# Hybrid attention and PEER block: the dense pass takes tiles 1 to 3 of the first half, and all four tiles of the second half are gathered

## The chip, the cores and the metric

The kernel runs on one core of a Trainium2 chip. The metric is the device time of one launch in microseconds, the median of three runs. A profiled execution of the same program gives the trace.

## The reference

One block of a decoder on 1024 tokens of width 1024: differential attention and a state-space mixer side by side, then a retrieval network (PEER) that picks 128 of 16384 single-neuron experts for each token. The change touches the retrieval network alone:

```python
q = (tb @ w_query).reshape(-1, 8, 2, 128)
sc = jnp.einsum('thjd,jkd->thjk', q, sub_keys)
val, idx = lax.top_k(sc, 16)
...
top_s, pos = lax.top_k(cand_s, 16)
eidx = jnp.take_along_axis(cand_i, pos, axis=-1)
g = jax.nn.softmax(top_s, axis=-1)
act = jax.nn.gelu(jnp.einsum('thkd,td->thk', expert_u[eidx], tb), approximate=False)
wts = g * act
return jnp.einsum('thk,thkd->td', wts, expert_v[eidx])
```

Then `x = layer_norm(ALPHA * x + gate2 * y_ffn, ln2_g, ln2_b)`.

## The kernel before

The 1024 tokens are taken in two halves of 512, each of four tiles of 128 tokens (tiles 0 to 3 and 4 to 7). `main` runs attention, the mixer, the projections and the first layer norm of the first half, then of the second; each half ends with `scores`, which multiplies by `w_query` and the sub-keys and writes the scores of all tiles to DRAM (`sc_d`).

After that a tile goes through `route`: VectorE searches the 16 best of each head (`top16`), adds candidates and picks experts by one-hot passes (`oh`, `fe`). Then a tile goes one of two ways.

A **gathered** tile (`gathered`): GpSimd gathers one row of `peer_u` per token for each of 128 selections (a u row: 128 tokens by 1024 values, 512 KB, tile `grow`), and VectorE multiplies it with the tokens' h2 and sums (line 1125). Then 128 v rows of `peer_v` are gathered, one for each token, and TensorE adds them up with the weights (`ps_y`). `finish` makes the last layer norm.

A **dense** tile: `spread` turns its experts and weights into a full table of gates, token by 16384 experts, as products of two one-hot rows (`first_k` on VectorE, `second_k` on GpSimd, `ps_gate` on TensorE), which goes to DRAM (`g_d`). `dense` then runs over all 128 blocks of 128 experts: `ps_u` with the block of `peer_u`, GELU, times the gates (`act_t`, read back as `gl`), and `ps_v` with the block of `peer_v`. One block is called a dense step here. Every weight is split into a high and a low part (`whi` on ScalarE, `wlo` on VectorE, line 220).

`few = 2, 3` says how many tiles of each half are gathered: tiles 0, 1 and 4, 5, 6; tiles 2, 3 and 7 are dense. The dense loop is `lead` = 12 steps ahead with `ps_u`; before the first multiplication with gates it issues all that is missing of the routing (`await_gates`), tile 7 coming first in the second half.

The order of work: `drive` records the main stream and after each piece of it as much of the other work as a credit allows (`ratio`, `ratio1`), gathering (`side`) and routing (`urgent`) by turns given in `share`. Every engine then executes its instructions in one fixed order, so an instruction that waits holds all behind it on its engine. Gathered rows lie in the `row` buffers (6, shared with scores, one-hots and norm rows) and, in the dense stage, in 7 `row2` buffers; `gs`, which collects gates for DRAM, has one buffer. A v row is multiplied `rows_by` = 4 rows after its gather was issued.

## Time and profile before

| | |
|---|---|
| median of three runs | 4839.74 us (4829.25 to 4852.5) |
| profiled execution | 4822.5 us, span 4820.7 us |
| TensorE busy | 4016.2 us (83%) |
| VectorE busy | 2974.3 us (62%) |
| ScalarE busy | 1423.7 us (30%) |
| GpSimd busy | 1881.6 us (39%) |
| DMA | 1134.14 MB, mean 235 GB/s |
| mean granted TensorE clock | 0.909 |

The span is the time from the first to the last instruction of the profiled execution. A share of busy time is a mean over stages that differ: the first half ends near 1100 us, the second half near 2540 us, the dense steps run from 3010 to about 4480 us, and the last gathered tile ends the program. So the time is read stage by stage.

### The profile page before, as it was taken

How to read it: one execution, taken by the hardware profiler on the slowest of the kernel's cores; microseconds unless marked ns; L12 is line 12 of the kernel's file. 1: busy time of each engine (PE TensorE's matmuls, PEld its weight loads, DVE VectorE, ACT ScalarE, POOL GpSimd, SP SyncE). 2: the span in 40 equal slices, each digit the busy share in tenths (PEclk: the TensorE clock that was granted, in tenths of full speed). 3: DMA queues.
4: the chain of work that ended last, by engine and by line, in shares of the span. 5: the costliest groups of instructions: out<-in, count | busy, mean ns of one | idle time of the engine just before them, and what ended most of it. 6: DMA issues, size and time to landing. Idle time of an engine off the chain costs nothing.

```text
span 4820.7 us, 52596 instructions
## 1 busy us (share of the span) xinstructions
PE 4016.2 (83%) x17996; PEld 2752.8 (57%) x17996; DVE 2974.3 (62%) x6965; ACT 1423.7 (30%) x2340; POOL 1881.6 (39%) x1720
## 2 busy tenths in 40 slices
...
GB/s 282 105 70 119 73 107 103 137 147 101 170 163 163 300 232 236 264 266 276 191 303 256 319 195 92 308 311 297 275 280 285 355 333 325 272 284 314 361 393 349
DMA packets 443648, 1134.14 MB, mean 235 GB/s; under 512 B 141852, under 2 KB 164532, under 8 KB 443380
## 3 DMA queue, kind: packets, MB, share of 16 engines
...
q8 instruction: 143, 2.34, 0.2%
q14 instruction: 125, 1.02, 0.1%
...
## 4 chain that ended last, share of the span: by engine, by line
PE 54%; DVE 18%; DMA 13%; issue 8%; POOL 5%; ACT 2%; SPq 1%; DVEq 0%; ACTq 0%; POOLq 0%
PE ps_u L269 9%; PE ps_v L1330 8%; PE ps_y L1290 7%; DVE grow L1125 5%; PE ps_x L269 5%; DMA grow<-in_peer_v,ej 5%; PE ps_b L269 4%; DMA grow<-in_peer_u,ei 3%; PE ps_z L269 3%; PE ps_g L269 2%; POOL grow L1182 2%; DVE wlo L220 2%; POOL second_k L1259 2%; PE ps_vT L269 2%; PE ps_pq L269 2%
## 5 line engine op out<-in xcount | busy, mean ns | idle before, releaser
L1182 POOL DMA_INDIRECT grow<-in_peer_u,ei x640 | 856.0, 1337 | 983.9 <-DVE grow L1125 312.0
L1182 POOL DMA_INDIRECT grow<-in_peer_v,ej x640 | 681.8, 1065 | 731.1 <-PE ps_y L1290 589.0
L219 ACT CAST whi<-wraw 128x1024 fp32r<-128x1024 f32 x498 | 519.9, 1047 | 1390.7 <-PE ps_u L269 548.9
L220 DVE TENSOR_TENSOR wlo<-wraw,whi 128x1024 fp32r<-128x1024 f32 x498 | 607.2, 1220 | 483.5 <-ACT whi L219 431.7
L1125 DVE SCALAR_TENSOR_TENSOR grow<-grow,gh 128x1024 f32<-128x1024 f32 x640 | 771.3, 1220 | 96.9 <-DMA grow<-in_peer_u,ei 95.4
L1290 PE MATMUL ps_y<-grow,own 128*32 128x512 f32 x2560 | 614.6, 636 | 83.7 <-DMA grow<-in_peer_v,ej 63.5
L269 PE MATMUL ps_u<-hhi,whi 128*128 128x384 f32 x1024 | 363.4, 355 | 48.2 <-ACT whi L219 40.8
L269 PE MATMUL ps_u<-hhi,wlo 128*128 128x384 f32 x1024 | 361.7, 353 | 44.2 <-DVE wlo L220 44.0
L1259 POOL TENSOR_SCALAR second_k<-iota_c,at 128x128 f32<-128x128 f32 x384 | 308.6, 814 | 228.3 <-PE ps_gate L1290 181.4
L983 POOL DMA_DIRECT2D h2s_d<-bighi x8 | 4.5, 561 | 915.3 <-ACT bighi L245 915.3
L1152 DVE COPY own<-wt 128x4 f32<-128x4 f32 x160 | 28.6, 182 | 536.5 <-PE ps_y L1290 532.7
L269 PE MATMUL ps_u<-hlo,whi 128*128 128x384 f32 x1024 | 354.9, 347 | 0.0
L1290 PEld LDWEIGHTS ps_y<-grow,own 128*32 128x32 f32 x2560 | 89.9, 111 | 405.7 <-DMA grow<-in_peer_v,ej 203.3
L1290 PE MATMUL ps_gate<-first_k,second_k 128*128 128x128 f32 x768 | 192.7, 386 | 107.7 <-POOL second_k L1259 62.0
L1330 PE MATMUL ps_v<-whi,ehi 128*128 128x512 f32 x768 | 225.2, 411 | 68.0 <-ACT whi L219 49.2
L1330 PE MATMUL ps_v<-wlo,ehi 128*128 128x512 f32 x768 | 256.4, 407 | 23.3 <-DVE wlo L220 23.3
L269 PEld LDWEIGHTS ps_u<-hhi,whi 128*128 128x128 f32 x1024 | 199.8, 195 | 118.2 <-ACT whi L219 52.3
L269 PEld LDWEIGHTS ps_u<-hhi,wlo 128*128 128x128 f32 x1024 | 199.7, 195 | 97.6 <-DVE wlo L220 65.8
L1330 PE MATMUL ps_v<-whi,elo 128*128 128x512 f32 x768 | 249.3, 400 | 0.0
L1290 PEld LDWEIGHTS ps_gate<-first_k,second_k 128*128 128x128 f32 x768 | 152.2, 250 | 157.7 <-POOL second_k L1259 102.4
L1330 PEld LDWEIGHTS ps_v<-whi,ehi 128*128 128x128 f32 x768 | 142.9, 193 | 128.3 <-ACT whi L219 59.9
L269 PEld LDWEIGHTS ps_u<-hlo,whi 128*128 128x128 f32 x1024 | 199.7, 195 | 17.8 <-issue 14.3
...
## 6 DMA issues: line engine op xcount, KB each, us to landing
wraw<-in_w_in SPq DMA_DIRECT2D x160, 512.0 KB, 3.7
wraw<-in_peer_uT SPq DMA_DIRECT2D x128, 512.0 KB, 6.3
wraw<-in_peer_v SPq DMA_DIRECT2D x128, 512.0 KB, 6.6
wada<-in_w_adaT SPq DMA_DIRECT2D x48, 512.0 KB, 6.6
g_d<-gs ACTq DMA_DIRECT2D x48, 512.0 KB, 4.3
gl<-g_d SPq DMA_DIRECT2D x48, 512.0 KB, 13.2
...
wraw<-in_w_ssd SPq DMA_DIRECT2D x32, 512.0 KB, 3.7
```

The lines of the kernel that those rows point to most:

```text
L219: nc.scalar.copy(hi, raw)
L220: i = nc.vector.tensor_tensor(lo, raw, hi.bitcast(F32), op=ALU.subtract)
L269: i = self.nc.tensor.matmul(ps, w[x][:, k, :], r[y][:, k, :], start=k + n == 0, stop=k == kk - 1 and n == 2)
L983: nc.gpsimd.dma_start(self.h2s_d[part][:, k, :], big[k][part][:, g0:])
L1125: nc.vector.scalar_tensor_tensor(u, u, 1.0, h2, op0=ALU.mult, op1=ALU.mult, accum_out=act[:, k : k + 1])
L1152: nc.vector.tensor_copy(own[:, :, OWN - 1].rearrange("p (h r) -> p h r", h=2), wt[:, b * n : b * n + n].rearrange("p (h r) -> p h r", h=2) ...
L1182: self.nc.gpsimd.indirect_dma_start(out=r, out_offset=None, in_=table, in_offset=bass.IndirectOffsetOnAxis(ap=ei[:, k : k + 1], axis=0),)
L1259: nc.gpsimd.tensor_scalar(second, self.iota_c, at[:, 1, k : k + 1], None, op0=ALU.is_equal)
L1290: return op(*args, **kw)
L1330: nc.tensor.matmul(acc[2 * tt + c], prev[x][:, tt * P : tt * P + P], v[y].rearrange("p k c -> p (k c)")[:, c * 512 : c * 512 + 512], start ...
```

## The change

Tiles 1, 2 and 3 are dense and tiles 0, 4, 5, 6 and 7 are gathered (`few = 1, 4`): the dense pass needs no tile of the second half. Routing of a half is planned before its scores, and `route` waits while recording until the scores it needs are recorded (`scored`). The dense loop is 2 steps ahead instead of 12. Gathered rows have buffers of their own, 4 in the two halves and 10 in the dense stage; the other rows share 4, `gs` and `ys` among them; `finish` and `rows_out` load their rows one by one, and h2 is made in place. Turns are one gathering to one routing step in the halves (two to one before), and a v row waits 2 rows in the halves and 6 in the dense stage. In DRAM the gates lie so that a load moves 4 KB runs and a write 256-byte runs; before it was the other way.

```diff
--- before.py
+++ after.py
@@ -48,22 +48,22 @@
 class Block:
     n_two = 12
     n_four = 5
-    n_row = 6
-    n_row2 = 7
-
-    lead = 12
+    n_row = 4
+    n_grow = 4, 10
+
+    lead = 2
     ahead = 1000000
-    ratio = 0.95
+    ratio = 0.9
     ratio1 = 1.1
 
-    share = 2, 4
+    share = 1, 4
     lag = 6, 2
 
     behind_by = 2
 
-    rows_by = 4
-
-    few = 2, 3
+    rows_by = 2, 6
+
+    few = 1, 4
     banks = {"pj0": 1, "pj1": 1, "ms": 2, "S": 3, "gate": 1}
 
     def __init__(self, ctx, tc, a, out):
...
@@ -132,7 +132,7 @@
         self.h2s_d = [dr.tile([P, KD, TH - P * self.few[0]], F32R, name=f"h2s_d{i}") for i in range(2)]
 
         self.g_d = {
-            hb * 4 + t: dr.tile([P, 16, P, 8], F32, name=f"g_d{hb * 4 + t}")
+            hb * 4 + t: dr.tile([P, 16, 16, 64], F32, name=f"g_d{hb * 4 + t}")
             for hb in range(2) for t in range(self.few[hb], 4)
         }
 
...
@@ -347,8 +347,9 @@
         self.mod2 = m
 
     def row(self, name):
-        if self.dp and name == "grow":
-            return self.dp.tile([P, D], F32, name=name, tag="row2", bufs=self.n_row2)
+        if name == "grow":
+            pool, n = (self.dp, self.n_grow[1]) if self.dp else (self.gp, self.n_grow[0])
+            return pool.tile([P, D], F32, name=name, tag="grow", bufs=n)
         return self.gp.tile([P, D], F32, name=name, tag="row", bufs=self.n_row)
 
 
...
@@ -966,36 +967,37 @@
             if b in (2, 4, 6):
                 yield from islice(fill, 1)
         yield from fill
-        rows = []
-        for src, off in ((a["ln1_g"], 0), (a["ln1_b"], 0), (self.mod_d, D), (self.mod_d, 0)):
-            rows.append(self.row("lnr"))
-            nc.sync.dma_start(rows[-1], bcast_rows(src, off, D))
-        self.late = v, rows
+        self.late_v = v
         self.h2T = self.join(big)
-        g0 = P * self.few[hb]
-        if hb:
-            for part in range(2):
-                for k in range(KD):
-                    nc.gpsimd.dma_start(self.h2x[part][:, k, TH - P * self.few[0] :], big[k][part][:, g0:])
-        else:
+        if hb == 0:
             for k in range(KD):
                 for part in range(2):
-                    nc.gpsimd.dma_start(self.h2s_d[part][:, k, :], big[k][part][:, g0:])
+                    nc.gpsimd.dma_start(self.h2s_d[part][:, k, :], big[k][part][:, P * self.few[0] :])
 
     def rows_out(self, hb):
 
-        nc = self.nc
-        v, rows = self.late
+        nc, a, v = self.nc, self.a, self.late_v
+
+        def load(*srcs):
+            rows = []
+            for src, off in srcs:
+                rows.append(self.row("lnr"))
+                nc.sync.dma_start(rows[-1], bcast_rows(src, off, D))
+            return rows
+
+        rows = load((a["ln1_g"], 0), (a["ln1_b"], 0))
         for tt in range(4):
             sl = slice(hb * TH + tt * P, hb * TH + tt * P + P)
             nc.vector.tensor_tensor(v[tt], v[tt], rows[0], op=ALU.mult)
             nc.vector.tensor_tensor(v[tt], v[tt], rows[1], op=ALU.add)
             nc.sync.dma_start(self.x1_d[sl, :], v[tt])
-            if tt < self.few[hb]:
-                h2 = self.row("h2")
-                nc.vector.tensor_tensor(h2, v[tt], rows[2], op=ALU.mult)
-                nc.vector.tensor_tensor(h2, h2, rows[3], op=ALU.add)
-                nc.sync.dma_start(self.h2_d[sl, :], h2)
+            yield
+        rows = load((self.mod_d, D), (self.mod_d, 0))
+        for tt in range(self.few[hb]):
+            sl = slice(hb * TH + tt * P, hb * TH + tt * P + P)
+            nc.vector.tensor_tensor(v[tt], v[tt], rows[0], op=ALU.mult)
+            nc.vector.tensor_tensor(v[tt], v[tt], rows[1], op=ALU.add)
+            nc.sync.dma_start(self.h2_d[sl, :], v[tt])
             yield
 
     def first_half(self):
...
@@ -1056,6 +1059,8 @@
         val, idx = small("val"), small("idx", U32)
         fi = idx.bitcast(F32)
         for half in range(2):
+            while self.scored < (tile_no // 4, 8 * half + 8):
+                yield 0.0
             s = self.row("scr").rearrange("p (a b) -> p a b", a=8)
             nc.sync.dma_start(s, self.sc_d[tile_no, :, half * 8 : half * 8 + 8, :])
             for i in range(8):
...
@@ -1136,13 +1141,14 @@
         self.claimed = False
 
         n = 2 * OWN
+        by = self.rows_by[self.dp is not None]
         rows = deque()
-        for k in range(P + self.rows_by):
+        for k in range(P + by):
             if k < P:
                 b, r, half = k // n, k % n // 2, k % 2
                 rows.append(self.gather(a["peer_v"], ej, b * n + half * OWN + r))
-            if k >= self.rows_by and k % 2:
-                j = k - self.rows_by
+            if k >= by and k % 2:
+                j = k - by
                 b, r = j // n, j % n // 2
                 if r == 0:
                     yield from self.claim("side")
...
@@ -1188,35 +1194,42 @@
     def finish(self, t0, y, src=None):
 
         nc, a = self.nc, self.a
-        x1, rows = self.row("gx1"), []
-        nc.sync.dma_start(x1, self.x1_d[t0 : t0 + P, :])
-        for r, off in ((self.mod_d, 2 * D), (a["ln2_g"], 0), (a["ln2_b"], 0)):
-            rows.append(self.row("gr2"))
-            nc.sync.dma_start(rows[-1], bcast_rows(r, off, D))
+
+        def load(src):
+            r = self.row("gr2")
+            nc.sync.dma_start(r, src)
+            return r
+
+        gate = load(bcast_rows(self.mod_d, 2 * D, D))
         if src is None:
-            nc.vector.tensor_tensor(y, y, rows[0], op=ALU.mult)
+            nc.vector.tensor_tensor(y, y, gate, op=ALU.mult)
         else:
             for c, ps in enumerate(src):
                 cs = slice(c * 512, c * 512 + 512)
-                nc.vector.tensor_tensor(y[:, cs], ps, rows[0][:, cs], op=ALU.mult)
-        nc.vector.scalar_tensor_tensor(y, x1, ALPHA, y, op0=ALU.mult, op1=ALU.add)
+                nc.vector.tensor_tensor(y[:, cs], ps, gate[:, cs], op=ALU.mult)
+        nc.vector.scalar_tensor_tensor(
+            y, load(self.x1_d[t0 : t0 + P, :]), ALPHA, y, op0=ALU.mult, op1=ALU.add
+        )
         mean, rs = self.moments([y], self.gp, "ln2")
-        nc.vector.scalar_tensor_tensor(y, y, mean, rows[1], op0=ALU.subtract, op1=ALU.mult)
-        nc.vector.scalar_tensor_tensor(y, y, rs, rows[2], op0=ALU.mult, op1=ALU.add)
+        nc.vector.scalar_tensor_tensor(
+            y, y, mean, load(bcast_rows(a["ln2_g"], 0, D)), op0=ALU.subtract, op1=ALU.mult
+        )
+        nc.vector.scalar_tensor_tensor(
+            y, y, rs, load(bcast_rows(a["ln2_b"], 0, D)), op0=ALU.mult, op1=ALU.add
+        )
         nc.sync.dma_start(self.out[t0 : t0 + P, :], y)
 
 
-    def routing(self, hb):
+    def routing(self, tiles):
 
         nc, gp = self.nc, self.gp
-        tiles = range(4 * hb, 4 * hb + 4)
-        for t in reversed(tiles) if hb else tiles:
-            while len(self.picked) == 3:
+        for t in tiles:
+            while len(self.picked) == 2:
                 yield 0.0
             yield from self.route(t)
             fe, g = self.routed
-            if t < 4 * hb + self.few[hb]:
-                ei, ej = [gp.tile([P, NSEL], I32, name=x, tag=x, bufs=3) for x in ("ei", "ej")]
+            if t % 4 < self.few[t // 4]:
+                ei, ej = [gp.tile([P, NSEL], I32, name=x, tag=x, bufs=2) for x in ("ei", "ej")]
                 nc.vector.tensor_copy(ei, fe)
                 yield from self.claim("urgent")
                 ps = self.psum("ps_ej", tag="gate")
...
@@ -1261,20 +1274,17 @@
             if k >= self.behind_by:
                 n = k - self.behind_by
                 if n % 4 == 0:
-                    spare = next(self.spare, None)
-                    if spare is None:
-                        yield from self.claim("urgent")
-                    ps = self.psum("ps_gate", tag=spare or "gate")
+                    yield from self.claim("urgent")
+                    ps = self.psum("ps_gate", tag="gate")
                 first, second = ready.popleft()
                 self.inline(nc.tensor.matmul, ps[:, n % 4 * P : n % 4 * P + P], second, first, start=True, stop=True)
                 if n % 8 == 0:
-                    gs = gp.tile([P, D], F32, name="gs", tag="gs", bufs=1).rearrange("p (i t) -> p t i", t=8)
+                    gs = self.row("gs").rearrange("p (i t) -> p t i", t=8)
                 if n % 4 == 3:
                     nc.scalar.copy(gs[:, n % 8 - 3 : n % 8 + 1, :], ps.rearrange("p (t i) -> p t i", t=4))
-                    if spare is None:
-                        self.claimed = False
+                    self.claimed = False
                 if n % 8 == 7:
-                    nc.scalar.dma_start(self.g_d[t][:, n // 8], gs.rearrange("p t i -> p i t"))
+                    nc.scalar.dma_start(self.g_d[t][:, :, n // 8], gs.rearrange("p t (b i) -> p b (i t)", b=16))
             if k % 2:
                 yield 1.0
 
...
@@ -1294,8 +1304,7 @@
         nc, a, dp = self.nc, self.a, self.dp
         tiles = list(self.g_d)
         n = P * len(tiles)
-        tags = ("S", "S", "S", "ms", "ms", "pj1")[: 2 * len(tiles)]
-        self.spare = cycle(tags)
+        acc = [self.psum("ps_v", tag=t) for t in ("S", "S", "S", "ms", "ms", "pj1")[: 2 * len(tiles)]]
         ts, prev = deque(), None
         for e in range(P + self.lead + 1):
             if e < P:
...
@@ -1309,14 +1318,15 @@
             if f < 0:
                 continue
             if f < P:
+                if f == 0:
+                    while self.missing:
+                        self.step("side" if self.claimed == "side" else "urgent")
                 if f % 8 == 0:
-                    if f == 0:
-                        self.await_gates()
-                        self.spare = iter(())
-                        acc = [self.psum("ps_v", tag=t) for t in tags]
                     gt = dp.tile([P, len(tiles) * 16, 8, 8], F32, name="gl", tag="gl", bufs=2)
                     for i, t in enumerate(tiles):
-                        nc.sync.dma_start(gt[:, i * 16 : i * 16 + 16], self.g_d[t][:, :, f : f + 8, :])
+                        nc.sync.dma_start(
+                            gt[:, i * 16 : i * 16 + 16].rearrange("p g i t -> p g (i t)"), self.g_d[t][:, f // 8]
+                        )
                 t = ts.popleft()
                 tv = t.rearrange("p (i t) -> p i t", t=8)
                 nc.vector.tensor_tensor(tv, tv, gt[:, :, f % 8, :], op=ALU.mult)
...
@@ -1376,9 +1381,9 @@
             else:
                 self.h2x = self.first_half()
             yield from self.post_norm(hb, big, fill)
+            self.scored = hb, 0
+            self.plan(hb)
             yield from self.scores(hb, self.h2T)
-            if hb == 0:
-                self.plan(0)
 
     def step(self, only=None):
 
...
@@ -1440,9 +1445,7 @@
 
     def plan(self, hb):
 
-        while self.urgent:
-            self.step()
-        self.urgent = self.routing(hb)
+        self.urgent = chain(self.urgent or (), self.routing(range(4 * hb, 4 * hb + 4)))
 
     def run(self):
         tc = self.tc
...
@@ -1461,10 +1464,7 @@
             self.wp = c.enter_context(tc.tile_pool(name="wp", bufs=1))
             with tc.tile_pool(name="bp", bufs=1) as self.bp, tc.tile_pool(name="mp", bufs=1) as self.mp:
                 self.drive(self.main(), self.ratio, self.lag[0])
-                while self.urgent:
-                    self.step()
             with tc.tile_pool(name="dp", bufs=1) as self.dp:
-                self.plan(1)
                 self.drive(self.dense(self.h2x), self.ratio1, self.lag[1])
                 while self.side or self.urgent:
                     self.step()
```

What GpSimd executes from tile 7's gates to the end, before: the first rows are the end of tile 1's v rows among tile 3's gates (`second_k`), then tile 7's gates, then three gathered tiles.

```order
L1182 DMA grow<-in_peer_v,ej 128x1024 x30
L1259 TENSOR_SCALAR second_k<-iota_c,at 128x128 x2
L1182 DMA grow<-in_peer_v,ej 128x1024 x2
L1259 TENSOR_SCALAR second_k<-iota_c,at 128x128 x6
L1182 DMA grow<-in_peer_v,ej 128x1024 x26
L1259 TENSOR_SCALAR second_k<-iota_c,at 128x128 x166
L1182 DMA grow<-in_peer_u,ei 128x1024 x128
L1182 DMA grow<-in_peer_v,ej 128x1024 x128
L1182 DMA grow<-in_peer_u,ei 128x1024 x128
L1182 DMA grow<-in_peer_v,ej 128x1024 x128
L1182 DMA grow<-in_peer_u,ei 128x1024 x128
L1182 DMA grow<-in_peer_v,ej 128x1024 x128
```

The same place after, from the v rows of tile 0 (`hhi` and `hlo` are the dense pass's tokens):

```order
L1188 DMA grow<-in_peer_v,ej 128x1024 x39
L1009 DMA hlo<-h2s_d_117 128x8x384
L1009 DMA hhi<-h2s_d_116 128x8x384
L1188 DMA grow<-in_peer_v,ej 128x1024 x85
L1272 TENSOR_SCALAR second_k<-iota_c,at 128x128 x128
L1188 DMA grow<-in_peer_u,ei 128x1024 x128
L1188 DMA grow<-in_peer_v,ej 128x1024 x128
L1188 DMA grow<-in_peer_u,ei 128x1024 x128
L1188 DMA grow<-in_peer_v,ej 128x1024 x128
L1188 DMA grow<-in_peer_u,ei 128x1024 x128
L1188 DMA grow<-in_peer_v,ej 128x1024 x128
L1188 DMA grow<-in_peer_u,ei 128x1024 x128
L1188 DMA grow<-in_peer_v,ej 128x1024 x128
```

The gates in front of the dense steps are now tile 3's, and four gathered tiles stand behind them instead of three.

TensorE at the same place, before: the last v products of tile 1 (`ps_y`), gates of tile 3, keys and gates of tile 7, then the first products with `peer_v`.

```order
L1290 MATMUL ps_y<-grow,own_103 32x512 x8
L1290 MATMUL ps_gate<-first_k,second_k 128x128 x40
L1290 MATMUL ps_key<-ident,keys 128x128 x2
L1290 MATMUL ps_key<-ident,g 128x128
L1290 MATMUL ps_gate<-first_k,second_k 128x128 x128
L1330 MATMUL ps_v<-whi,ehi 128x512 x2
L1330 MATMUL ps_v<-wlo,ehi 128x512 x2
L1330 MATMUL ps_v<-whi,ehi 128x512 x2
L1330 MATMUL ps_v<-wlo,ehi 128x512 x2
```

TensorE after, where keys and gates of tile 3 stand behind the first block of `ps_u`:

```order
L269 MATMUL ps_u<-hhi,whi 128x384
L269 MATMUL ps_u<-hlo,whi 128x384
L269 MATMUL ps_u<-hhi,wlo 128x384
L1300 MATMUL ps_key<-ident,keys 128x128 x2
L1300 MATMUL ps_key<-ident,g 128x128
L1300 MATMUL ps_gate<-first_k,second_k 128x128 x128
L269 MATMUL ps_u<-hhi,whi 128x384
L269 MATMUL ps_u<-hlo,whi 128x384
L269 MATMUL ps_u<-hhi,wlo 128x384
L269 MATMUL ps_u<-hhi,whi 128x384
```

The products of a gathered tile no longer stand there; tile 0's are now spread over the end of the second half's main stream. On VectorE the u rows of a tile stand before among 24.5 and 26 dense steps (tiles 6 and 5) and now among 19, 16.5 and 16.5 (tiles 4, 5 and 6), the route of the following tile with them each time.

## Rows read from the trace of the kernel before

**Rows 1.** Windows by stage: us, busy time (instructions) of PE, PEld, DVE, ACT, POOL.

```profile
1100.00:1500.00 400.00, 353.22 (x1501) 238.56 (x1500) 388.50 (x1318) 168.69 (x353) 80.58 (x68) 0.88 0.43 139
1500.00:2100.00 600.00, 569.83 (x2702) 363.26 (x2700) 366.97 (x685) 236.40 (x384) 308.13 (x283) 0.97 0.73 248
2100.00:2540.00 440.00, 322.41 (x1482) 258.09 (x1483) 365.32 (x844) 112.42 (x145) 265.59 (x240) 0.84 0.80 263
2540.00:3010.00 470.00, 313.31 (x1250) 167.88 (x1250) 201.11 (x755) 78.88 (x88) 255.74 (x324) 0.71 0.62 217
3010.00:3400.00 390.00, 304.18 (x1376) 253.49 (x1375) 357.12 (x882) 100.96 (x137) 200.46 (x143) 0.93 0.90 300
3400.00:3700.00 300.00, 291.72 (x1342) 172.16 (x1342) 84.95 (x127) 67.21 (x93) 127.07 (x110) 0.99 0.85 288
3700.00:4050.00 350.00, 295.46 (x1392) 249.18 (x1391) 262.89 (x408) 95.18 (x131) 203.56 (x140) 0.93 0.95 334
4050.00:4390.00 340.00, 339.61 (x1557) 200.92 (x1556) 89.24 (x129) 75.41 (x104) 142.95 (x127) 1.00 0.83 283
4390.00:4640.00 250.00, 96.96 (x409) 74.30 (x408) 211.65 (x373) 28.68 (x40) 163.55 (x133) 0.70 0.95 356
4640.00:4821.00 181.00, 128.28 (x490) 18.38 (x488) 13.51 (x47) 2.34 (x4) 109.42 (x117) 0.94 0.93 368
```

**Rows 2.** PE's waits, 2000 to 2400 us: in total, times, longest.

```profile
PE ps_key L1290 <- DVE ln1t L238: 31.5, 1, 31.5
```

**Rows 3.** PE's timeline at the handover: start, duration, idle time before in brackets.

```profile
2898.47 0.71 PE L1290 MATMUL ps_key<-ident,keys 128*128 128x128 f32 x2 [30.94 <-DVE keys L1242]
2953.24 37.32 PE L1290 MATMUL ps_gate<-first_k,second_k 128*128 128x128 f32 x130 [0.87 <-POOL second_k L1259]
3018.96 0.33 PE L269 MATMUL ps_u<-hhi,whi 128*128 128x384 f32 x1
3027.27 0.33 PE L269 MATMUL ps_u<-hhi,whi 128*128 128x384 f32 x1
```

**Rows 4.** Windows of line 1290's matmuls, second half, and of ps_y, tail.

```profile
1100.00:2540.00 1440.00, 197.43 (x895) 82.97 (x896) 0.90 0.67 222
4390.00:4821.00 431.00, 134.54 (x512) 19.48 (x512) 0.00 (x0) 2.34 (x4) 0.80 0.94 361
```

**Rows 5.** Groups of VectorE by form: busy us, mean ns, idle time before.

```profile
L1125 DVE SCALAR_TENSOR_TENSOR grow<-grow,gh 128x1024 f32<-128x1024 f32 x640 | 771.3, 1220 | 96.9 <-DMA grow<-in_peer_u,ei 95.4
L220 DVE TENSOR_TENSOR wlo<-wraw,whi 128x1024 fp32r<-128x1024 f32 x498 | 607.2, 1220 | 483.5 <-ACT whi L219 431.7 <-PE ps_u L269 29.6 <-PE ps_v L1330 11.1
L1322 DVE TENSOR_TENSOR act_t<-act_t,gl 128x384 f32<-128x384 f32 x128 | 69.6, 552 | 63.2 <-ACT act_t L1305 49.7 <-DMA gl<-g_d 12.8
L322 DVE SCALAR_TENSOR_TENSOR wada<-wada,cs 128x512 f32<-128x512 f32 x96 | 67.6, 741 | 4.5 <-DMA wada<-in_w_adaT 4.5
L1097 DVE TENSOR_TENSOR oh<-pos,iota_c 128x800 f32<-128x800 f32 x64 | 61.0, 985 | 0.1
L1125 DVE DVE_READ_ACCUMULATOR grow<-grow,gh 128x1 f32 x640 | 51.0, 80 | 0.0
L1018 DVE FIND_INDEX8 idx<-val,tkw 128x8 uint32<-128x128 f32 x128 | 35.6, 282 | 0.0
```

**Rows 6.** The chain that ended last: first u row after tile 7's gates.

```profile
3044.73 8.41 DMA grow<-in_peer_u,ei
```

**Rows 7.** DMA issues: count, KB each, median us to landing.

```profile
wraw<-in_peer_uT SPq DMA_DIRECT2D x128, 512.0 KB, 6.3
g_d<-gs ACTq DMA_DIRECT2D x48, 512.0 KB, 4.3
gl<-g_d SPq DMA_DIRECT2D x48, 512.0 KB, 13.2
```

**Rows 8.** The chain that ended last, 3380 to 3480 us: SP at a gate load.

```profile
3434.50 9.15 SPq L1319
```

**Rows 9.** Groups of GpSimd: the u gathers and their idle time before.

```profile
L1182 POOL DMA_INDIRECT grow<-in_peer_u,ei x640 | 856.0, 1337 | 983.9 <-DVE grow L1125 312.0 <-DMA k<-kT_d 206.7 <-issue 94.9
```

14 lines of the change are left out of this document (6 added, 8 removed).

## The prediction

> **What bounds the kernel now.** I read the windows by stage first. From 1100 us (the end of the first half's scores) to 2540 us TensorE is busy 353 + 570 + 322 = 1245 of 1440 us [rows 1]: the second half is held by TensorE, with 195 us idle, 47 of them where VectorE is at 388 of 400 us (attention beside three tiles' routing) and 118 in the last 440 us, where tile 1's u rows, tile 3's routing and the norm share VectorE. One wait there is 31.5 us for routing keys [rows 2]. From 2540 to 3010 us nothing fills an engine; the granted clock is 0.71, a mix of TensorE's two levels (1.2 and 2.4 GHz). The dense loop stands still until tile 7 is routed and its gates are made: the keys come at 2898.47, after a 30.94 us wait, the last gate ends at 2953.24 + 37.32 = 2990.6 [rows 3]. Then the stages alternate. While u rows are gathered (3010 to 3400, 3700 to 4050) VectorE is busy 357 of 390 and 263 of 350 us and DMA 0.90 to 0.95; while v rows are gathered (3400 to 3700, 4050 to 4390) TensorE is busy 292 of 300 and 340 of 340 us [rows 1]. After 4390 us the last tile's rows run nearly alone.
>
> Prices in that part. One dense step (24 ps_u, 18 ps_v) takes 3027.27 - 3018.96 = 8.31 us of TensorE with nothing beside it [rows 3]; a tile's 512 ps_y records take 134.5 us at the low clock of the tail [rows 4], and I take 125. On VectorE a u row costs 1.220 + 0.080 = 1.30 us, so 128 cost 166; a dense step costs two weight residues at 1.22 and two passes at 0.55, 3.54 us; a route costs 24 one-hot passes of 0.98 (three lines like the one shown) and 80 searches of 0.28 (five lines like the one shown), 46 us, and I take 60 for the shorter searches and sums around them [rows 5]. A gathered row is 0.524 MB, a dense step moves two weights and 3/8 of a gate load, 1.25 MB.
>
> These prices give the kernel before back. The order of VectorE's work puts 24.5 dense steps beside tile 6's u rows, 22.5 beside its v rows, then 26 and 24 for tile 5, and 9.5 between. Tile 6's u: 166 + 1.4 routes (84) + 87 = 337. Tile 5's u has no route, so DMA decides: 99.6 MB at 334 GB/s, 298. The v stretches are 22.5 and 24 steps of 8.31 plus 125: 312 and 324; between: 79. Sum 1350; the trace has 4390 - 3044.7 [rows 1, 6] = 1345.
>
> **The change, part by part.** The number of dense and of gathered tiles stays (three, five), so the totals of every engine stay; what moves is when.
>
> Second half. Tile 1's 128 u rows (166 us of VectorE) leave it, as do its 67 MB; tile 0's 512 ps_y records stay; tile 2's gates stay, tile 1's come in whole where a part of tile 3's left. The side matmuls were 895 records in 197 us [rows 4], 0.22 each; 512 + 512 records make 1024, 29 us more. The idle time I put from 195 to 90: 25 of the 47 us beside the attention (one route less there; route 0 starts inside the scores of the first half), 70 of the 118 at the end (no u rows, no keys wait), 10 between. Net -76, so the scores end at 2464. From both sides: nothing gained, 2569; all idle gone, 2374.
>
> Handover. In the order only tile 3's gates remain, behind one ps_u group: TensorE then waits for the rest of route 3 (some 18 one-hot passes, 18 us) and 128 gates, which took 2990.6 - 2898.5 = 92 us for tile 7 [rows 3]. Gates done: 2464 + 18 + 92 = 2574, 417 earlier than before. The queue behind that wait is the rest of TensorE's dense work; lead 2 instead of 12 costs little, as only 10 ps_u groups (some 4 us each) are moved behind it.
>
> Gate runs. A gate load moves 512 KB and lands in 13.2 us (256-byte runs) where a weight of the same size takes 6.3, and issuing one held SP for 9.15 us [rows 7, 8]. After, the load goes in 4 KB runs and the write in 256-byte runs. I cost the load's gain at nothing, because the u stretches will be VectorE's and the v stretches TensorE's; if VectorE had room it is 3 x 7 us of latency per 8 steps, all prefetched. The write took 4.3 us [rows 7]; 16 of them at no more than a load's 13.2 us, now from four rotating buffers instead of one, lie inside 92 us of gates if they overlap. The trace shows no 256-byte write; I take no cost on the path, and the other end is a rival below. The Trainium skill, DMA: Bandwidth & Descriptors, Specifications, says that transfers below 512 B make the DMA engine read, modify and write; it speaks against moving the short runs to the writing side; no run here shows such a write, and by the rule the sum would be that of the rival on short writes.
>
> First row. After tile 3's gates VectorE still owes 16 row passes (x1, h2: 16 x 1.22 = 20), route 4 (60) and about 5 dense steps (18): 98 us to tile 4's first u row. Before it was 3044.7 - 2990.6 = 54 [rows 3, 6], since route 6 ran beside tile 7's gates. SP holds the h2 stores, gate loads and weights behind those passes; dense steps wait with it.
>
> Dense loop with three gathered tiles inside it instead of two. The order puts 19, 16.5 and 16.5 steps beside the u rows of tiles 4, 5, 6, each with one route: 166 + 60 + 58 to 67 = 284 to 293 us of VectorE; DMA would want 88 to 91 MB, 263 to 272 us at 334 GB/s, so VectorE is last. It was busy 357 of 390 us in such a stretch [rows 1], so I add a little: 300 + 292 + 292 = 884. The v stretches take 55 steps and three tiles: 457 + 375 = 832; between them 14.5 steps, 120. Sum 1836. This is the extra tile: 1836 against 1345.
>
> Tail. Tile 7 starts when the dense steps are over: 67 MB at 356 GB/s, 188, a turn of 12, then 181 as before [rows 1]: 381 instead of 431.
>
> The start loads w_ada through four buffers instead of six; VectorE waited 4.5 us for it in all [rows 5], so 0 to 10 us, taken as nothing.
>
> Sum: 2574 + 98 + 1836 + 381 = 4889 against a span of 4821 (profiled execution 4822.5): +68. The median of the runs is 4839.74, 17 above the profiled one; carried over, 4908.
>
> **Rivals.** *Even.* The second half sheds 140 instead of 76 us, because idle falls to 26. For: 600 us of it already run with TensorE busy 570 us. Against: the norm and attention leave idle time in it that no side work causes. 4908 - 64 = 4844.
> *Faster.* The u stretches run at 250 us, as tile 4's did from 4390 to 4640 us [rows 1], because ten buffers instead of seven and long-run gate loads keep rows coming, and routing slips into the v stretches, where VectorE is busy 85 of 300 us. For: POOL sat 312 us waiting for VectorE to free rows [rows 9]. Against: the order has each route among the u rows. 884 - 750 = 134 less: 4774. It decides once a stretch falls below about 264 us.
> *Writes in short runs.* If each 256-byte write lasts 13.2 us and the next waits for it, the gates take 16 x 13.2 = 211 instead of 92, and the second half's 32 writes hold ScalarE's copies too: 5027 and up. For: ScalarE both copies the gates and issues the writes, in one queue with the weights' casts. Against: four buffers for the gates instead of one. (This is how the rule of the Trainium skill's DMA page would show here.)
> *The change does not do what it says* (dense still waits for routing of the second half): the order excludes it, the only gates in front of the dense steps are tile 3's.
>
> **How the numbers follow.** About 0.5% (24 us) is what a measurement of this kernel can tell from no change. Forecast, 4865 to 4960: 0.47. Short writes: 0.15. Even: 0.20. Faster: 0.18. So slower 0.62, same 0.20, faster 0.18. The forecast's own spread is -76 +/- 50 in the second half and +/- 15 per u stretch. The range takes in the even case, the near half of the faster one and the near half of the writes: 4785 to 5020, which leaves out about 0.09 and 0.08.
>
> **What would show it.** Scores ending between 2420 and 2500 us; 90 to 110 us from the keys to the last gate, or 200 if the writes hold it; u stretches of 285 to 305 us with VectorE above 90%; v stretches of some 277 us with TensorE full; a tail near 380. It is wrong if u stretches are DMA-bound at 250 us, or if the second half ends before 2400 us.

## The result, and the profile after

The changed kernel takes 4876.65 us (median of five runs, 4868.43 to 4881.5), the kernel before in the same comparison 4840.62 us (five runs, 4829.25 to 4852.5). The ratio is 1.0069, 95% interval 1.0046 to 1.0091: 36 us slower, where 68 were forecast. The profiled execution took 4879.0 us with a span of 4877.3 us, 56.6 us longer than the span of before (4820.7).

The stages of the changed kernel, in windows cut at the events that the prediction used (columns as in [rows 1]):

```profile
core 0: us, PE busy (x) PEld busy (x) DVE busy (x) ACT busy (x) POOL busy (x), PEclk, DMA share, GB/s
1100.00:1500.00 400.00, 351.05 (x1585) 243.63 (x1584) 345.36 (x1083) 181.55 (x366) 142.34 (x130) 0.89 0.43 129
1500.00:2100.00 600.00, 522.15 (x2539) 411.69 (x2537) 463.54 (x1087) 276.92 (x441) 261.94 (x262) 0.89 0.56 169
2100.00:2489.00 389.00, 374.02 (x1645) 209.29 (x1646) 157.19 (x414) 70.83 (x89) 128.40 (x122) 0.98 0.77 259
2489.00:2624.00 135.00, 82.43 (x284) 64.54 (x283) 66.02 (x159) 35.15 (x34) 78.11 (x128) 0.53 0.35 85
2624.00:2717.60 93.60, 54.63 (x260) 48.52 (x261) 89.78 (x316) 22.88 (x31) 4.88 (x5) 0.80 0.54 185
2717.60:2974.20 256.60, 183.16 (x785) 154.67 (x784) 252.89 (x541) 57.00 (x78) 182.69 (x130) 0.91 0.96 358
2974.20:3327.70 353.50, 338.87 (x1566) 202.59 (x1565) 98.97 (x168) 75.39 (x107) 135.88 (x132) 0.99 0.85 301
3327.70:3573.60 245.90, 173.70 (x701) 145.63 (x700) 245.90 (x546) 52.13 (x71) 175.01 (x127) 0.87 0.95 353
3573.60:3904.90 331.30, 327.91 (x1537) 196.17 (x1537) 100.38 (x174) 73.48 (x103) 136.98 (x130) 1.00 0.87 314
3904.90:4153.60 248.70, 174.77 (x722) 147.68 (x720) 247.59 (x546) 53.68 (x73) 176.31 (x126) 0.88 0.95 350
4153.60:4471.70 318.10, 289.56 (x1333) 162.15 (x1333) 77.77 (x123) 58.45 (x82) 142.64 (x131) 0.96 0.84 297
4471.70:4877.30 405.60, 125.37 (x513) 19.71 (x513) 190.19 (x374) 2.92 (x6) 272.17 (x246) 0.70 0.93 348
```

Three rows are the second half, two the handover, then the last stage: u stretch, v stretch by turns, and the last tile. A u stretch goes from a tile's first u row to its last, a v stretch from there to the next tile's first u row. In tile 5's u stretch VectorE is busy 245.90 of 245.90 us; in its v stretch TensorE is busy 327.91 of 331.30 us; in the last 405.60 us TensorE has 125.37 us of work.

Where the stages begin is read from the products of the scores (line by tile: duration min/median/max in ns, first and last start) and from the u rows. Of before:

```profile
L1038 PE MATMUL ps_sc<-keysT,pq x256: 270/275/422, 1005.3 to 2504.4; 128*128 128x128 f32 x128
```

```profile
L1125 DVE SCALAR_TENSOR_TENSOR grow<-grow,gh x128: 1171/1211/1226, 3048.6 to 3369.4; 128x1024 f32<-128x1024 f32 x128
```

And of after, where tile 4's u rows come first:

```profile
L1040 PE MATMUL ps_sc<-keysT,pq x256: 270/275/552, 999.5 to 2488.7; 128*128 128x128 f32 x128
```

```profile
L1130 DVE SCALAR_TENSOR_TENSOR grow<-grow,gh x128: 1168/1208/1254, 2717.6 to 2973.0; 128x1024 f32<-128x1024 f32 x128
```

The scores end only 16 us earlier (2504.4, 2488.7), the first u row comes 331 us earlier (3048.6, 2717.6). What follows it in the two kernels, as one window each, before first:

```profile
3048.60:4820.70 1772.10, 1417.63 (x6375) 934.70 (x6373) 985.77 (x1893) 353.47 (x486) 942.69 (x765) 0.92 0.90 318
```

```profile
2717.60:4877.30 2159.70, 1613.33 (x7150) 1028.60 (x7148) 1213.68 (x2466) 373.05 (x517) 1221.66 (x1019) 0.90 0.90 329
```

The last stage is 388 us longer: 388 - 331 = 57, the difference of the two spans. It moves 2159.7 x 329 = 711 MB instead of 1772.1 x 318 = 564; a gathered tile is 134 MB of it. The tile came out of the second half, where DMA was busy 0.43, 0.73 and 0.80 [rows 1], into a stage where it is at 0.90.

### The profile page after: what moved, and what is told of

The parts are those of the page before. It is cut to its first block, busy times and chain, and to the rows that moved or that the text cites. A ratio compares the mean times of both kernels' runs of the same rounds, so it can differ in the third digit from the quotient of the medians.

```text
span 4877.3 us, 52557 instructions
## 1 busy us (share of the span) xinstructions
PE 4001.2 (82%) x17996; PEld 2769.0 (57%) x17996; DVE 2976.9 (61%) x6965; ACT 1419.5 (29%) x2340; POOL 1862.1 (38%) x1704
## 4 chain that ended last, share of the span: by engine, by line
PE 52%; DVE 22%; DMA 9%; issue 8%; POOL 6%; ACT 2%; SPq 0%; ACTq 0%; POOLq 0%; DVEq 0%
PE ps_y L1300 9%; DVE grow L1130 7%; PE ps_u L269 7%; PE ps_v L1340 6%; PE ps_b L269 5%; DMA grow<-in_peer_u,ei 4%; PE ps_x L269 4%; DVE wlo L220 3%; PE ps_z L269 3%; PE ps_g L269 3%; POOL grow L1188 3%; PE ps_pq L269 3%; POOL second_k L1272 3%; PE ps_vT L269 2%; PE ps_o L269 2%
## 5 line engine op out<-in xcount | busy, mean ns | idle before, releaser
L1188 POOL DMA_INDIRECT grow<-in_peer_u,ei x640 | 834.0, 1303 | 765.4 <-DVE ei L1233 199.8
L1300 PE MATMUL ps_y<-grow,own 128*32 128x512 f32 x2560 | 580.7, 620 | 67.8 <-issue 28.7
L1272 POOL TENSOR_SCALAR second_k<-iota_c,at 128x128 f32<-128x128 f32 x384 | 321.7, 847 | 493.0 <-PE ps_gate L1300 303.8
L269 PE MATMUL ps_u<-hhi,wlo 128*128 128x384 f32 x1024 | 383.6, 375 | 138.3 <-DVE wlo L220 138.3
L269 PE MATMUL ps_u<-hhi,whi 128*128 128x384 f32 x1024 | 378.9, 370 | 66.6 <-ACT act_t L1314 52.5
L269 PE MATMUL ps_u<-hlo,whi 128*128 128x384 f32 x1024 | 370.2, 362 | 0.0
L269 PEld LDWEIGHTS ps_u<-hhi,wlo 128*128 128x128 f32 x1024 | 212.4, 207 | 215.2 <-DVE wlo L220 162.5
L269 PEld LDWEIGHTS ps_u<-hhi,whi 128*128 128x128 f32 x1024 | 212.6, 208 | 133.6 <-ACT act_t L1314 63.5
L1300 PE MATMUL ps_gate<-first_k,second_k 128*128 128x128 f32 x768 | 176.4, 360 | 85.8 <-POOL second_k L1272 59.1
L1340 PEld LDWEIGHTS ps_v<-wlo,ehi 128*128 128x128 f32 x768 | 142.0, 193 | 118.6 <-DVE wlo L220 51.2
```

What stands on the lines that cost most here:

```text
L269: i = self.nc.tensor.matmul(ps, w[x][:, k, :], r[y][:, k, :], start=k + n == 0, stop=k == kk - 1 and n == 2)
L1188: self.nc.gpsimd.indirect_dma_start(out=r, out_offset=None, in_=table, in_offset=bass.IndirectOffsetOnAxis(ap=ei[:, k : k + 1], axis=0),)
L1272: nc.gpsimd.tensor_scalar(second, self.iota_c, at[:, 1, k : k + 1], None, op0=ALU.is_equal)
L1300: return op(*args, **kw)
L1340: nc.tensor.matmul(acc[2 * tt + c], prev[x][:, tt * P : tt * P + P], v[y].rearrange("p k c -> p (k c)")[:, c * 512 : c * 512 + 512], start ...
```

## The experiments

Times are medians of four runs (a_spare eight, b_few14ng ten), with the ratio to the kernel before and its 95% interval. The kernel before, run in each comparison, had medians of 4833 to 4843 us there. So a difference of less than some 10 us between kernels of two comparisons says nothing. "a_" kernels start from the changed kernel, "b_" kernels from the one before.

### Which part of the change costs

**The two halves of the change.** The old choice of tiles in the changed kernel (with the dense tokens taken from both halves, and tile 7 routed first, as before), and the new choice in the kernel before:

```diff
 a_few23 (after)
-    few = 1, 4
+    few = 2, 3
 b_few14 (before)
-    few = 2, 3
+    few = 1, 4
```

> The changed kernel with the old choice of tiles (tiles 0, 1, 4, 5, 6 gathered; 2, 3, 7 dense, tile 7 routed first), everything else of the change kept. Theory: the 36 us come from the choice of tiles, an extra cycle of a VectorE-held u stretch (246 us) and a v stretch with what lies between (about 335) that a handover 367 us earlier and 25 us less of tail do not pay for. Then this kernel is within 15 us of before, 4825 to 4856, and again has a standstill of over 80 us for tile 7's keys and gates. Rival: the choice of tiles is even, and the other edits cost (four shared rows, two rows of prefetch in the halves, norm rows one by one, short gate writes). Then this kernel is at 4877 or above.

> The kernel before with the new choice of tiles alone (few = 1, 4; a copy that would be empty is left out). Theory: slower than before by 20 to 90 us (4860 to 4930), with three u and v cycles in the dense stage. Rival (the other edits cost): 4845 or below, faster than the changed kernel by 30 us or more.

a_few23 took 4878.5 us (ratio 1.0092, 1.0060 to 1.0125), b_few14 4878.6 us (1.0104, 1.0075 to 1.0133). Each half of the change alone costs 45 us, both together 36. So the choice of tiles does cost, as b_few14 says, but it is not the whole: the first theory's number for a_few23 is missed and the rival's holds. In a_few23 the stretch from the end of the scores to the first u row of the last stage is long and thin:

```profile
2530.00:3250.00 720.00, 462.20 (x1847) 282.29 (x1848) 337.16 (x972) 137.10 (x158) 341.67 (x411) 0.73 0.59 191
```

The dense loop starts there at 3030 us, but tile 6's u rows only at 3250, 200 us later than before. In the trace tile 1's v products run from 2734 to 3161 us, behind tile 3's gates and on both sides of tile 7's; before they ran from 2550 to 2820, beside tile 3's gates. After tile 1's last gather GpSimd stands 108 us until tile 6's first. Which of the other edits makes it so was not taken further.

**Gate runs.**

```diff
 a_oldgate (after); b_newgate is the reverse on before
-    dr.tile([P, 16, 16, 64], F32, ...)
+    dr.tile([P, 16, P, 8], F32, ...)
...
-    dma_start(self.g_d[t][:, :, n // 8], gs.rearrange("p t (b i) -> p b (i t)", b=16))
+    dma_start(self.g_d[t][:, n // 8], gs.rearrange("p t i -> p i t"))
...
-    dma_start(gt[...].rearrange("p g i t -> p g (i t)"), self.g_d[t][:, f // 8])
+    dma_start(gt[...], self.g_d[t][:, :, f : f + 8, :])
```

> The changed kernel with the gates in DRAM as before: written in 4 KB runs, loaded in 256-byte runs. Theory: the gate's runs move nothing on the path, within 12 us of the changed kernel (4865 to 4889), gate writes near 4.3 us, loads near 13 us. Rival one, the short writes cost: 20 us or more faster, with less than 100 us from tile 3's keys to its last gate instead of 117. Rival two, the long loads pay: 20 us or more slower, with longer u stretches than 246 to 257 us.

> The kernel before with the gates laid out as in the changed kernel: loaded in 4 KB runs, written in 256-byte runs. In the changed kernel with the old layout a load's issue held SP for 3.8 us (median) instead of 0.43, and weights came late to VectorE (24.6 and 11.4 us of waits in two u stretches). Theory: the same here, 15 to 35 us faster than before (4800 to 4820). Rival, the gain hangs on VectorE being last in the u stretches of the changed kernel, or the short writes cost: within 10 us of before, or slower.

a_oldgate took 4904.2 us (1.0152, 1.0118 to 1.0186), 27 us more than the changed kernel; b_newgate 4782.6 us (0.9892, 0.9873 to 0.9911), 54 less than before. The long loads pay, more than expected on the kernel before. In a_oldgate, gate loads on SP (duration of the issue, min/median/max in ns), and VectorE's longest wait and ScalarE's wait for a weight in the first u stretch (total, times, longest):

```profile
L1327 SPq DMA_DIRECT2D gl<-g_d x48: 529/3828/14618, 2652.5 to 4224.9; - x48
```

```profile
DVE wlo L220 <- ACT whi L219: 24.6, 4, 14.0
```

```profile
ACT whi L219 <- DMA wraw<-in_peer_v: 17.2, 3, 15.8
```

The same loads in the changed kernel, and its gate writes of the handover on ScalarE's queue:

```profile
L1327 SPq DMA_DIRECT2D gl<-g_d x48: 320/426/1247, 2653.5 to 4189.5; - x48
```

```profile
L1287 ACTq DMA_DIRECT2D g_d<-gs x16: 520/521/543, 2516.9 to 2624.9; - x16
```

A short-run load holds SP for 3.83 us (median; 14.6 at most) instead of 0.43. The weights are behind it in SP's queue; they come late to ScalarE's cast, and VectorE, in order, stands 24.6 us in a stretch where it is last: that u stretch lasts 286 us instead of 257. The short-run writes hold ScalarE's queue 0.52 us each; the long-run writes of before held it 0.33 (median). The new choice of tiles with long loads, and nothing else of the change:

> The kernel before with the new choice of tiles and gates loaded in 4 KB runs, nothing else of the change. Theory: SP, held 3.8 us by each short-run gate load, costs in any choice of tiles, so this lies 25 to 55 us under the new choice alone (4879): 4824 to 4854, and the rest of the change (fewer shared rows, one bank for gates, shorter lead, other turns) costs 25 to 50 us net of its ten buffers. Rival: the long loads gain only where three tiles are gathered in the last stage; then 4865 or above, and the rest of the change is even.

It took 4847.6 us (1.0020, 1.0006 to 1.0033; ten runs, 4830 to 4865), 31 us under b_few14: the theory's range. The rest of the change costs 29 us net on top of it (4876.65). So the way from before to after has three steps: the long loads give 54 us (b_newgate), the choice of tiles costs 65 on top of them (b_few14ng against b_newgate, 4847.6 and 4782.6), and the rest costs 29. That makes 40, where the comparison of the two kernels shows 36.

**Buffers of gathered rows.**

```diff
 a_grow7 (after)
-    n_grow = 4, 10
+    n_grow = 4, 7
 a_behind8 (after)
-    n_grow = 4, 10
+    n_grow = 4, 9
...
+        op, by = (self.dp, 8) if self.dp else (gp, self.behind_by)
...
-        for k in range(P + self.behind_by):
+        for k in range(P + by):
...
-    bufs=self.behind_by + 1
+    bufs=by + 1
```

> The changed kernel with 7 instead of 10 buffers for gathered rows in the dense stage. Theory: VectorE sets the u stretches and TensorE the v stretches, so it is within 12 us of the changed kernel. Rival: the ten buffers are what brought the u stretches to 250 us; then they grow by 10 us or more each, and the whole by over 30 us.

> The changed kernel with nine buffers instead of three for each of the two one-hot rows of a gate in the dense stage (nine buffers for gathered rows instead of ten make the room). Theory: tile 3's gates take 117 us from the keys because GpSimd's second one-hot row and TensorE's product run in lock-step through three buffers (2.39 us of TensorE and 1.21 us of wait per four); with nine, GpSimd sets the pace at 2.45 us per four: 78 to 88 us from keys to last gate, and 20 to 38 us faster (4840 to 4858). Rival: after the gates VectorE's row passes and route 4 are late anyway, so the first u row moves by under 8 us and the time stays within 12 us of the changed kernel.

a_grow7 took 4921.8 us (1.0191, 1.0167 to 1.0215), 45 us slower: the theory fell. The edit of a_behind8 missed its aim. Tile 3's gates are recorded in the second half, ahead of the dense stage, and keep the three buffers; in its trace four gates still take 3.60 us; what was left is a kernel with 9 buffers for gathered rows, and it took 4897.9 us (1.0131, 1.0100 to 1.0161), 21 slower. The buffers act at least in part through the order that the scheduler writes. In VectorE's order the dense steps beside the u and v rows of tiles 4, 5, 6 are 19, 25, 16.5, 24.5, 16.5, 20 with ten buffers, 19, 27.5, 17.5, 27, 18, 12.5 with nine, 24, 30.5, 22, 32.5, 12.5, 0 with seven. With fewer buffers more steps go beside the early rows, the steps run out sooner, and a longer end runs with TensorE nearly idle. In a_grow7 from the last ps_v to the end:

```profile
4205.00:4500.00 295.00, 134.30 (x514) 19.85 (x514) 95.86 (x201) 4.51 (x8) 196.40 (x181) 0.80 0.93 336
4500.00:4911.50 411.50, 134.06 (x513) 20.17 (x513) 192.09 (x376) 2.92 (x6) 267.96 (x249) 0.71 0.93 348
```

Over 706 us, the end of tile 6 and the whole of tile 7, TensorE has 268 us of work and DMA is at 0.93; in the changed kernel such an end is 432 us long (from 4445).

**The bank for gates, and the lead.**

```diff
 a_spare (after)
-                    yield from self.claim("urgent")
-                    ps = self.psum("ps_gate", tag="gate")
+                    if t != 3:
+                        yield from self.claim("urgent")
+                    ps = self.psum("ps_gate", tag="S" if t == 3 else "gate")
...
-                    self.claimed = False
+                    if t != 3:
+                        self.claimed = False
 a_lead6 (after)
-    lead = 2
+    lead = 6
```

> The changed kernel with tile 3's gates made in three PSUM banks by turns (those of attention, idle by then) instead of the one bank that the change leaves for gates. Theory: in the handover TensorE's four products (2.39 us) and ScalarE's copy of the bank (1.08 us) take turns, 3.60 us per four; before, with six spare banks, GpSimd's second one-hot row at 0.58 us set the pace. So tile 3's gates take 76 to 90 us instead of 115, and the kernel is 20 to 38 us faster (4839 to 4857). Rival: VectorE's row passes and route 4 hold the first u row anyway: first u row within 10 us of 2717, time within 12 us of the changed kernel.

> The changed kernel with the dense loop 6 steps ahead instead of 2. Prediction's reading: only four more ps_u groups of about 4 us go ahead of the wait for gates, 0 to 16 us faster (4861 to 4877). Rival: a longer lead evens out waits of the whole dense loop, 25 us or more faster.

a_spare took 4857.1 us (1.0039, 1.0023 to 1.0055; eight runs), 20 us under the changed kernel and at the near end of the theory's range; its first u row comes at 2686.2, 31 us earlier. The handover of the changed kernel, from its timeline (start, duration, idle time before):

```profile
2558.66 1.18 POOL L1272 TENSOR_SCALAR second_k<-iota_c,at 128x128 f32<-128x128 f32 x2
2558.96 1.08 ACT L1284 COPY gs<-ps_gate 128x512 f32<-128x512 f32 x1 [2.52 <-PE ps_gate L1300]
...
2560.13 2.39 PE L1300 MATMUL ps_gate<-first_k,second_k 128*128 128x128 f32 x8 [1.21 <-POOL second_k L1272]
...
2562.56 1.08 ACT L1284 COPY gs<-ps_gate 128x512 f32<-128x512 f32 x1 [2.52 <-PE ps_gate L1300]
...
2563.74 2.38 PE L1300 MATMUL ps_gate<-first_k,second_k 128*128 128x128 f32 x8 [1.22 <-POOL second_k L1272]
```

And of a_spare, GpSimd at the same work:

```profile
2513.65 75.91 POOL L1272 TENSOR_SCALAR second_k<-iota_c,at 128x128 f32<-128x128 f32 x128 [59.04 <-ACT at L1262]
```

The trace names GpSimd as what TensorE waited for, and its rows were done at 2559.84. But TensorE starts at 2560.13, 0.09 us after ScalarE's copy of the bank ended (2558.96 + 1.08 = 2560.04), and again at 2563.74, 0.10 after the next. With one bank products and copy take turns, 3.60 us per four gates; with three, 128 of GpSimd's rows run without a gap in 75.91 us. The Trainium skill, Perfetto Trace Analysis, Matmuls, says that independent groups of matmuls should rotate through banks so that emptying one overlaps the next; the two traces agree, 115 us against 76. a_lead6 took 4875.2 us (1.0080, 1.0063 to 1.0098), the changed kernel's time within 2 us: the prediction's reading of the lead holds.

### What sets the stretches

```diff
 a_nohot (after), in route, ahead of the three one-hot passes of a head
+            if tile_no >= 4:
+                nc.vector.tensor_copy(fe[:, h, :], ci[:, h, 0:16])
+                yield 2.5
+                continue
```

> The changed kernel without the 24 one-hot passes in the routes of tiles 4 to 7; eight small copies take the first 16 candidates of each head instead, so that part of the selection is left out. VectorE's instructions start 0.9 to 1.15 us apart there, so a route loses about 22 us. Theory, VectorE sets the u stretches: those of tiles 4, 5, 6 go from 257, 246, 249 us to 225 to 238, and the first u row comes some 20 us earlier; in all 60 to 95 us faster (4780 to 4817). Rival, DMA is as late (0.95 busy, 350 GB/s): stretches stay over 242 us, and only the 20 us ahead of the first row are gained (4850 to 4862).

It took 4779.0 us (0.9907, 0.9877 to 0.9937), 98 us less. The stretches of tiles 5 and 6 in its trace:

```profile
3262.80:3496.60 233.80, 169.16 (x720) 143.59 (x719) 228.84 (x531) 51.71 (x70) 187.33 (x124) 0.90 0.97 368
3842.40:4076.40 234.00, 172.32 (x726) 147.01 (x725) 230.11 (x534) 52.58 (x71) 181.48 (x123) 0.88 0.96 364
```

They fall from 245.90 and 248.70 us to 234 with VectorE still at 0.98: VectorE is last, though with DMA at 0.96 there is little behind it. The first u row comes at 2676.8 instead of 2717.6, more than the 20 us expected. Tile 4's stretch is 261 us, not shorter, since 23 instead of 19 dense steps lie in it. Of the 102 us between the two spans 41 lie ahead of the first u row, 23 in the three u stretches, and 38 in the v stretches and the last tile, which neither reading named.

### Spreading the dense steps

The changed kernel has 25, 24.5 and 20 dense steps beside v rows, where TensorE is last, and none in the last tile. The next kernels put each piece of a dense step behind the gathering recorded two pieces earlier (`sided` holds the last gathering instruction on VectorE and on TensorE). b_pace has the same edit on b_newgate with `ratio1` 0.82, b_few14p on b_few14ng with `ratio1` 1.1 as it was. The two credit lines below are those of u rows; a v row's is 0.8 instead of 1.2:

```diff
 a_pace (after)
+            if self.dp:
+                marks.append(dict(self.sided))
+                if len(marks) > 2:
+                    mark = marks.popleft()
+                    for i in insts[n:]:
+                        if mark.get(i.engine):
+                            self.behind(i, mark[i.engine])
...
-            yield 1.2
+            yield 1.0 if self.dp else 1.2
```

> The changed kernel with the dense steps held back too: in the dense stage each piece of a dense step is placed behind the gathering recorded two pieces earlier, on VectorE and TensorE, and a u row counts 1.0, a v row 0.8 of credit instead of 1.2. VectorE's order then has 19, 19, 18.5 and 15 dense steps beside the u rows of tiles 4 to 7 (before 19, 16.5, 16.5, 0) and 13.5, 13, 14 and 11.5 beside or behind their v rows (before 25, 24.5, 20, 0). Theory: an extra cycle is dear because the v stretch is crowded with dense steps (25 x 8.31 + 115 us of TensorE) while the last tile has none. Then u stretches stay at 245 to 260 us, v stretches fall from about 285 to 235 to 250, and the last tile takes 460 to 490 instead of 406: 4700 to 4780, 100 us or more under the changed kernel and under the kernel before. Rival: DMA at 0.85 to 0.95 busy is as late, so spreading gives less than 40 us (over 4835).

> The kernel before with gates loaded in 4 KB runs and with the dense steps held back as in a_pace (credit for a dense step 0.82 instead of 1.1, so that the dense steps reach into the last tile). VectorE's order has 30.5, 20, 20 dense steps beside the u rows of tiles 6, 5, 4 and 19.5, 17, 7.5 beside their v rows. Theory: the price of the choice of tiles hung on how dense steps lie in the gathering stages; with steps spread in both, three cycles behind a late handover and four behind an early one end within 30 us of each other: 4670 to 4730 here (a_pace 4702), 55 to 110 us under the same kernel without the spreading (4783). Rival: the early handover pays by itself; then this is at 4745 or above.

> The same with the dense steps held back as in a_pace (21.5, 20, 14.5 and 15 dense steps beside the u rows of the four tiles, 15, 12.5, 12.5 and 10.5 beside or behind their v rows). Theory: the choice of tiles moves 134 MB of gathering from a stage where DMA is busy 0.6 to one where it is at 0.95, while the second half ends only some 20 us earlier, and so costs 30 to 50 us also with spread steps: 4695 to 4715 against 4664 of b_pace. Rival: with steps spread the choice is even and the other edits cost the 38 us between a_pace and b_pace: 4650 to 4680.

a_pace took 4701.7 us (0.9724, 0.9706 to 0.9741), 175 less than the changed kernel; b_pace 4664.0 us (0.9652, 0.9636 to 0.9668); b_few14p 4704.1 us (0.9726, 0.9710 to 0.9743). The spreading is worth 119 us to b_newgate and 144 to b_few14ng. b_pace came out 6 us under its theory's range, and 38 us from a_pace where 30 had been the most. Tile 4's u and v stretch and tile 7's in a_pace:

```profile
2722.30:2983.30 261.00, 186.48 (x783) 155.39 (x784) 253.45 (x542) 57.11 (x77) 188.38 (x128) 0.89 0.94 345
2983.30:3225.70 242.40, 210.13 (x1101) 119.31 (x1099) 59.08 (x126) 44.78 (x62) 139.01 (x134) 0.97 0.98 385
4234.80:4455.40 220.60, 150.16 (x609) 130.28 (x610) 198.48 (x325) 41.87 (x58) 177.72 (x122) 0.84 0.97 371
4455.40:4710.40 255.00, 185.88 (x1002) 104.77 (x1000) 77.38 (x158) 36.28 (x52) 127.76 (x125) 0.88 0.90 348
```

The u stretch is 4 us longer; the v stretch with what follows falls from 353.5 to 242.4 us, and the last tile takes 476 instead of 406, as expected. DMA is at 0.90 to 0.98 there. Over the three tiles ahead of the last the v stretches lose 276 us and the u stretches gain 35, the last tile gains 70. With steps spread, the choice of tiles costs 40 us (b_pace against b_few14p, which differ in `ratio1` too) and all other edits nothing (b_few14p against a_pace, 2 us). The last stage of b_pace, then of b_few14p:

```profile
3058.00:4657.70 1599.70, 1327.45 (x6313) 926.60 (x6311) 983.25 (x1895) 351.01 (x480) 957.02 (x763) 0.95 0.94 352
```

```profile
2660.00:4701.00 2041.00, 1560.57 (x7144) 1038.16 (x7144) 1210.12 (x2434) 380.91 (x520) 1259.38 (x1023) 0.91 0.94 350
```

At nearly the same rate the stage of b_few14p moves 714 instead of 563 MB: it is 441 us longer, and it begins 398 us earlier. That is the choice of tiles in two rows.

**The turns between tiles.** In a_pace VectorE waits for the last norm of each tile ahead of the next tile's u rows (total, times, longest):

```profile
DVE gy L1205 <- DMA gr<-mod_d: 89.3, 4, 25.9
```

```diff
 a_pace_fin (a_pace), in gathered, among the u rows
+            if k == 12 and self.late_y:
+                self.finish(*self.late_y)
+                self.late_y = None
...
 a_pace_fin2 (a_pace); b_pace9_fin has it on b_pace9
+            if self.late_y and k == 6:
+                y = self.row("gy")
+                nc.sync.dma_start(y, self.y_d[self.late_y[1]])
+            if self.late_y and k == 18:
+                self.finish(self.late_y[0], y)
+                self.late_y = None
...
```

a_best1 is a_pace_fin with the banks of a_spare and `n_grow` 4, 12; b_pace9 is b_pace with `n_row2` 9.

> a_pace with the last layer norm of tiles 4, 5 and 6 placed 12 u rows into the next tile instead of ahead of it. In a_pace VectorE stands 89 us in four waits of some 22 us for the rows of that norm, ahead of each next tile's u rows. Theory: three of these waits go, 35 to 65 us faster than a_pace (4637 to 4667). Rival: DMA is at 0.95 and 360 GB/s over the whole stage of a_pace and is what is late: less than 20 us faster (over 4682).

> a_pace_fin with the three banks of a_spare and 12 buffers for gathered rows instead of 10. If the three add up: 4595 to 4650. If DMA is the bound from the first u row on, only the handover's 25 to 35 us come on top of a_pace_fin, and the buffers give nothing.

> b_pace with 9 instead of 7 buffers for gathered rows. If DMA's rate is what holds the last stage of b_pace (0.94 busy, 352 GB/s), within 10 us of it (4654 to 4674). If rows wait for buffers there (three of them were worth 45 us in the changed kernel), 15 to 40 us faster.

a_pace_fin took 4697.1 us (0.9724, 0.9697 to 0.9751), 5 less than a_pace, as the rival had it. But the waits had not gone, they had moved. VectorE in its trace:

```profile
DVE val L1016 <- DMA scr<-sc_d: 48.1, 2, 24.6
...
DVE grow L1133 <- DMA gh<-h_d: 22.9, 1, 22.9
```

These are 71 us for the next route's scores and the next tile's h2, both loaded by SP behind the load of y, which waits for y to be written. So nothing was yet decided for DMA. a_best1 took 4681.4 us (0.9691, 0.9672 to 0.9711), 16 less than a_pace_fin and as expected by neither reading. b_pace9 took 4652.3 us (0.9620, 0.9604 to 0.9636), 12 under b_pace, between what its two readings expected.

> a_pace_fin with y of tiles 4 to 6 loaded 6 u rows into the next tile and its norm 18 rows in, so that the loads of the next tile's h2 and scores no longer lie on SP behind a load that waits for y. Theory, the turns between tiles: 71 us of waits of VectorE go, 30 to 60 us faster than a_pace_fin (4637 to 4667). Rival, DMA's rate (0.94, 360 GB/s) holds the stage: within 15 us of 4697.

> b_pace9 with the same edit for tiles 6 and 5. Theory, the turns: two waits of some 20 us go, 20 to 40 us faster than b_pace9 (4612 to 4632). Rival, DMA's rate: within 10 us of 4652.

With y loaded behind the scores and h2, a_pace_fin2 took 4659.2 us (0.9635, 0.9597 to 0.9674), 38 less than a_pace_fin, and b_pace9_fin 4601.9 us (0.9520, 0.9481 to 0.9560), 50 less than b_pace9, more than the 20 to 40 expected. It was the turns: DMA's rate was not yet the limit, it rose. The last stage of b_pace9_fin:

```profile
3050.00:4596.00 1546.00, 1321.57 (x6377) 931.71 (x6376) 993.03 (x1941) 355.58 (x487) 967.36 (x768) 0.96 0.96 367
```

The row shows 367 GB/s, where b_pace had 352 and b_pace9 356. b_pace9_fin is the fastest found, 4.8% under the kernel before, with the old choice of tiles.

## Why the prediction came out as it did

Direction right, size about twice: 68 us forecast, 36 measured. The step that failed is the price of the u stretches. VectorE was rightly named as what holds them, but its work was priced by adding up the durations of its records: 884 us for three stretches that took 751. That the sum still ends within 12 us of the measured span (4889, 4877.3) is luck: four other terms, the second half, the handover, the v stretches and the tail, were together 126 us too cheap. Of the 31 us between 4908 and 4876.65 the sum made some 12; the other 20 come from the last step, which carried the profile's distance from the median (17 us) over to the changed kernel. The profile of before was at the fast end of its runs (4822.5; the five runs are 4829 to 4852), the changed kernel's own lies 2.4 us above its median.

| term | predicted | measured |
|---|---|---|
| scores end | 2464 | 2489 |
| to the last gate | 18 + 92 | 135 |
| to the first u row | 98 | 94 |
| three u stretches | 884 | 256.6 + 245.9 + 248.7 = 751 |
| v stretches and between | 832 + 120 | 353.5 + 331.3 + 318.1 = 1003 |
| tail | 381 | 406 |

**Second half: 25 us short.** The scores of before ended at 2504.4, not at 2540 as the sum took it; what [rows 1] shows up to 2540 is norm rows, gathering and gates behind them. So the shedding was forecast from a wrong end, and it was 16 us, not 76 (and not the 140 of the rival *Even*). Before, up to the end of the scores:

```profile
1100.00:2504.40 1404.40, 1233.34 (x5632) 849.62 (x5630) 1097.19 (x2800) 511.44 (x875) 628.31 (x567) 0.91 0.66 221
```

TensorE is idle there for 171 us, and for 142 in the changed kernel; the prediction took 105 away. In the part from 2100 us on the idle time fell as expected (94 to 15 us), but from 1500 to 2100 us it grew from 30 to 78: with a routing step in every second turn VectorE's work there rose from 367 to 464 us, and TensorE's longest waits there are for tile 2's keys (18.0 us) and for `second_k` (16.2).

**Handover: 25 us short.** The 18 us to the keys were right; from the keys to the last gate it took 117 us, not 92. The 92 us of [rows 3] were made with six spare banks; the change takes these out, in plain sight of the diff, and the prediction let the price stand. With three banks a_spare takes 78. The rival on short writes is refuted at the same place: four gates take 3.60 us whether a write is issued or not, and the last write lands 4.15 us after its issue (the chain that ended last, of the changed kernel):

```profile
2624.90 4.15 DMA g_d<-gs
```

In [rows 7] a write in long runs took 4.3. The rule cited there, of transfers under 512 B, shows no price in this write.

**First row: right**, 94 for 98.

**u stretches: 133 us too long.** The prediction summed durations, 1.22 + 0.08 us for a u row. VectorE's records overlap. In the changed kernel's timeline:

```profile
3399.32 1.20 DVE L1130 SCALAR_TENSOR_TENSOR grow<-grow,gh 128x1024 f32<-128x1024 f32 x1
3400.45 0.08 DVE L1130 DVE_READ_ACCUMULATOR grow<-grow,gh 128x1 f32 x1
3400.45 1.22 DVE L1130 SCALAR_TENSOR_TENSOR grow<-grow,gh 128x1024 f32<-128x1024 f32 x1
3401.60 0.08 DVE L1130 DVE_READ_ACCUMULATOR grow<-grow,gh 128x1 f32 x1
3401.60 1.22 DVE L1130 SCALAR_TENSOR_TENSOR grow<-grow,gh 128x1024 f32<-128x1024 f32 x1
```

The next one starts while the last is still being recorded: 3400.45, 3401.60, one row per 1.15 us, and the accumulator read takes no time of its own. By spacing a tile's rows cost 147 instead of 166 us; the small instructions of a route, some 0.28 us each by their records, overlap likewise. The durations of all VectorE records that start in the three stretches add up to 859 us, close to the 861 that the prediction had before it added "a little"; by their starts they fit into 751. The little, 23 us for waits, did not come either: VectorE is idle for 5 us in the three. With short-run loads it would have (a_oldgate: 286, 248 and 264 us, with as much work of VectorE). The bound named (VectorE full) was right, its size not. The Trainium skill, Vector Engine (DVE) Microarchitecture Reference, Measured stream behaviour on trn2, gives 1.04 ns per column and some 75 ns per instruction; 1024 columns make 1.14 us, an estimate from that page, and the trace agrees with 1.15.

So the u stretches of the rival *Faster*, 250 us, came true, but not its reason: the routes stayed among the u rows, and VectorE holds them, as a_nohot shows. The prediction's own sign of being wrong, u stretches of 250 us that DMA holds, is met in the length alone. The time of *Faster* (4774) did not come, since the terms that were too cheap stand in it too. This is the more useful part: the check on before, 1350 against 1345, had passed with the same prices. By the events of its trace the two u stretches of before took 609 us where 635 stood, the v stretches with what follows 758 where 715 stood, and the end of it, tile 4's first u row, is at 4415.9 us and not at 4390.

**v stretches: 51 us too short.** In tile 4's v stretch the v rows themselves keep TensorE busy for 112 us (in the next two 112 and 108), not for 125:

```profile
2974.20:3327.70 353.50, 111.78 (x512) 17.16 (x512) 0.00 (x0) 2.35 (x4) 0.99 0.85 301
```

The 134.5 us of [rows 4] were not those of a low clock: nearly all of the 512 records stand behind 4640 us, where the granted clock is 0.94 [rows 1]. TensorE is idle for 15, 3 and 29 us of the three stretches. That leaves 625 of 1003 us for 69.5 dense steps, some 9.0 us each where 8.31 stood, a price taken with nothing beside the step. Why a step is dearer beside v rows is open. Most of the 29 us lie ahead of tile 7's first u row, when no dense step is left and VectorE stands for tile 6's last norm:

```profile
DVE gy L1205 <- DMA gr<-mod_d: 22.4, 1, 22.4
```

The rows of that norm stand on SP behind the load of y, which SP issues only at 4457.10, after a wait for y to be written. This wait was not taken out in the changed kernel itself; a_pace_fin2 against a_pace prices three such turns at 43 us.

**Tail: 25 us too short.** Tile 7's u rows took 198 us where 188 stood, and what follows 207 where 193 stood. Why is open.

**Load's gain at nothing: wrong.** That full engines would hide it did not hold: the weights stand behind the gate loads on SP, and a late weight stops the very VectorE that was said to hide it. a_oldgate says 27 us. The prediction had the 9.15 us of SP in [rows 8] in its hand (the median of these loads before is 3.46) and did not ask who stands behind it.

What stays open: why the other edits cost 96 us with the old choice of tiles (b_newgate against a_few23) and 29 with the new; and how the 45 us of the buffers split between the order and the gathering itself.
